# Trainium2: a two-layer transformer trunk whose context part of queries and keys is split first, with the first layer's convolution taps queued behind the query and key chains and the scores of two query tiles issued in turn by parts

## The chip, the cores and the metric

The kernel runs on one core of one Trainium2 chip. The metric is the device time of one execution in microseconds. Engines are named as in the profile: PE is TensorE (matmuls; PEld its weight loads), DVE is VectorE, ACT is ScalarE, POOL is GpSimd, SP is SyncE, which issues most of the DMAs. Each engine works through its own instructions in program order.

## The reference, cut to what matters

Two layers over 256 latent tokens and 256 context tokens of width 1024, all in fp32:

```
h, hc = modulate(rmsnorm(x)), modulate(rmsnorm(ctx))
p, pc = h @ w_in, hc @ w_in                  # GLU | q, k, v | gates
q, k = rope_2d(q), rope_2d(k)                # latent tokens only
conv = (silu(layernorm(dwconv31(glu(p))))) @ w_conv_out
attn = softmax(q k^T over a window + bias, and q k_ctx^T) v  @ w_na_out
x = x + g1 * (sigmoid(gates) . (conv, attn)) @ w_out
x = x + g2 * conv_ffn(modulate(rmsnorm(x)))
# layer 0 does the same for the context; layer 1 only needs its k and v
```

The result must agree with fp32, so every fp32 operand of a large product is split into a high part in the fp32r format and a low part (the rest): three matmuls, high x high, high x low and low x high, stand for one.

## The kernel before, in words

Tokens lie along the free axis (256 latent, then 256 context: 512 columns), channels on the 128 partitions. A "group" is one 128 x 512 output block: eight weight blocks times three matmuls, lines L197 to L199, 24 matmuls of 512 columns. Weights come by SP's DMA (`raw`), and are split on ACT into `whi` (L167 or L216) and on DVE into `wlo` (L168), or for some units of layer 0 on ACT and POOL (L217, L218). There are four buffers of each, so a split for the unit four later can begin when a group has ended. Four PSUM banks (`main`) take group results; two banks `sc`, one `pt` and one `po` belong to the attention.

The mixing half of layer 0 works in this order on PE: query group, key group, two GLU groups; then for each further head pair j = 1, 2, 3 the two GLU groups, the query and the key group; then the 16 gate groups. Between the groups a helper steps through the attention. For a head pair these are the score matmuls of two query tiles (L495), the softmax (L516 adds the bias and takes the maximum on DVE, L519 is the exponential and L522 the scaling on ACT, L521 the reciprocal on DVE), the transposes of the probabilities (L561 on PE, copied out of PSUM by ACT, L564, or L567 for the context), and the products with the values (L578, L587), whose result ACT and DVE split (L595, L596). In layer 0 there are also, after every second pair, the scores of the context's own queries with their softmax (L530, L535, L537, L540).

A query or key "chain" is the DVE and ACT work between a group's end and the scores: two reads of PSUM (L859, L860), the rotation (L861, then L864 for a query, L869 for a key), and splits into high (L881, ACT) and low (L882, DVE). In layer 0 and for keys there is a part that needs no rotation, the context's half of the columns (`qk<-main`).

The depthwise convolution is done on DVE by "taps": 31 instructions for each of four channel blocks, L671 the first and L673 the rest, each adding one shifted, weighted copy to `cb`. They are filler: `conv_run` hands out `rate` of them in each slot, a slot being half a group, in program order between the other work. `conv_tap` puts each behind the DVE instruction in `after[0]`, which before is the latest L516 (or L530). Once all taps are done, DVE adds the four blocks (L949, L950, L951), PE sums them over the channels (L955) and the LayerNorm follows. From the middle of the gate groups on DVE also computes dot products for the modulation (L304).

The score product of one tile is three matmuls for each of two heads, that is three parts:

```
for n, (a, b) in enumerate(((0, 0), (0, 1), (1, 0))):
    for o, r in zip(out, HALF):
        pe.matmul(o, q[r, a, c], runs(k[r, b, d]), start=n == 0, stop=n == 2)
```

with a, b = 0 for the high and 1 for the low part. The two heads use half of the rows each and run side by side.

Of the kernel before, what the change touches and what calls it, by code (L numbers as in the profile page):

```python
# [19 lines left out]
S = 256  # L20
GW = 64
# [32 lines left out]
def trunk(ctx: ExitStack, tc: tile.TileContext, xt, cvec, crow, wall, wada, params, bias_t, rope_t, out):  # L54
    nc = tc.nc
    pe, act, dve, pool, sp = nc.tensor, nc.scalar, nc.vector, nc.gpsimd, nc.sync
# [11 lines left out]
    def nm(s):  # L68
        uid[0] += 1
        return f"{s}_{uid[0]}"  # L70
# [3 lines left out]
    def psum(tag="main"):  # L74
        return psp.tile([P, 512], F32, tag=tag, bufs=BANKS[tag], name=nm(tag))
# [13 lines left out]
    def add_side(gen):  # L89
        side.append(gen)  # L90
# [23 lines left out]
    start = ExitStack()  # L114
# [70 lines left out]
    def runs(a):  # L185

        return a.rearrange("p (r c) -> p c r", r=2)
# [235 lines left out]
    class Attention:  # L423
# [61 lines left out]

        def issue(self):
            _, what, its = self.todo.pop(0)
            outs = [self.products(it, [psum(t) for t in tags]) for it, tags in zip(its, (("sc", "sc"), ("pt", "main")))]
            self.soft.append((what, its, [(self.scores if what == LAT else self.ctx_scores)(it, o) for it, o in zip(its, outs)]))

        def product(self, out, q, k, c, d):

            for n, (a, b) in enumerate(((0, 0), (0, 1), (1, 0))):
                for o, r in zip(out, HALF):
                    pe.matmul(o, q[r, a, c], runs(k[r, b, d]), start=n == 0, stop=n == 2)  # L495

        def products(self, it, out):
            j, qt, q, k, bt = it
            if qt is not None:
                d = slice(0, NS_) if qt else slice(KL, KN)  # L500
                self.product([ps[:, :NS_] for ps in out], q, k, slice(qt * P, (qt + 1) * P), d)
            else:
                for t in range(2):
                    self.product([ps[:, t * S : (t + 1) * S] for ps in out], q, k, slice(S + t * P, S + (t + 1) * P), KCTX)
            return out

        def scores(self, it, out):
            qt, bt = it[1], it[-1]
# [123 lines left out]
    for l in range(DEPTH):  # L632
        last = l == DEPTH - 1
# [4 lines left out]
        with ExitStack() if last else start as e1a:  # L638
# [74 lines left out]
            with ExitStack() as e1b:  # L713
# [123 lines left out]
                    glu_groups(1)  # L837

                conv = conv_run()
                rate[0] = 3 if last else 2.0  # L840
                add_side(conv)

                def qk(j):

                    att.ahead(j - 2)
                    bt = eb.tile([P, 5, NS_ // 2], F32, tag="bias", bufs=2 if last else 1, name=nm("bias"))
                    both = []
                    for what in range(2):
                        w = T if what == 0 else 2 * S
                        sc = HD ** -0.5 if what == 0 else 1.0  # L850
                        ps = in_group((T_Q, T_K)[what] + j, slice(0, w))
                        if what == 0:
# [7 lines left out]
                        dve.stream_shuffle(part(r2[:, LAT]), lat, SWAP16)  # L860
                        dve.tensor_tensor(r2[:, LAT], r2[:, LAT], rope[:, 1, :], ALU.mult)  # L861
                        if what == 0:
                            rq = tmp()
                            dve.tensor_tensor(  # L864
                                rq[:, LAT].rearrange("p (b r c) -> p b r c", b=NB_, r=ROWS),
                                blocks(r1[:, LAT]), blocks(r2[:, LAT]), ALU.add,
                            )
                        else:
                            dve.tensor_tensor(r1[:, LAT], r1[:, LAT], r2[:, LAT], ALU.add)  # L869
                        f = eb.tile([P, 2, KN if what else w], F32R, tag="qk"[what], bufs=2, name=nm("qk"))  # L870
                        if what == 0:
                            to = [([f[:, a, LAT] for a in range(2)], rq[:, LAT])]
                            if T > S:
                                to.append(([f[:, a, CTX] for a in range(2)], ctx_))
                        else:
                            rv_ = r1[:, LAT].rearrange("p (r c) -> p r c", r=ROWS)
                            to = [([f[:, a, KCTX] for a in range(2)], ctx_)]
                            for d, c in ((slice(0, KL), slice(GW - TC, GW)), (slice(KX, KN), slice(0, TC))):
                                to.append(([f[:, a, d].rearrange("p (c r) -> p r c", r=ROWS) for a in range(2)], rv_[:, :, c]))
                        for (hi, lo), src in to:  # L880
                            act.activation(hi, src, AF.Identity, scale=sc)  # L881
                            end = dve.scalar_tensor_tensor(lo, src, sc, hi.bitcast(F32), ALU.mult, ALU.subtract)  # L882
                        both.append(f)
                    att.pair(j, *both, bt, end)

                if l == 0:
                    for t in range(4):
                        keep_v(t, pv[t])
                    qk(0)
                    arun = att.run()  # L890
                    add_side(arun)
                    for j in range(1, 4):
                        glu_groups(j)
                        qk(j)
                        rate[0] = 3
                else:
                    glu_groups(2)
                    rate[0] = 3
                    wvs = [wunit(l, U_V + uu) for uu in range(4)]
                    for half in range(2):  # L900
                        pv = {t: psum() for t in (2 * half, 2 * half + 1)}
                        for k in range(KD):
                            v_tile(pv, wvs[k // 2], k, pv)
                            if k % 2:
                                slot()
                        for t, p in pv.items():
                            keep_v(t, p)
                    qk(0)
                    glu_groups(3)
                    arun = att.run()  # L910
# [446 lines left out]
```

## Time and profile before

| what | value |
|---|---|
| median of 3 runs | 1056.82 us (1056.28 to 1058.88) |
| the profiled execution, its own time | 1054.58 us |
| its span, first to last instruction | 1052.8 us |
| granted TensorE clock, mean | 0.997 |
| busy: PE, DVE, ACT, POOL | 1032.4, 893.2, 565.6, 43.7 us |
| taps: L673 240 times, L671 8 times | 144.7 us for L673 |
| layer 0's mixing half, roughly | 50 to 300 us |
| layer 1's mixing half, roughly | 690 to 850 us |

In a timeline row the first number is the start in microseconds from the span's start, the second the time to the end of the row's last instruction, x the number of instructions merged, and the bracket the idle time of the engine ahead of it with the instruction that ended it. A row of several instructions in a chain gives their spacing.

### The profile page before, as it was taken

What the parts mean: (1) busy time and instruction counts of PE and PEld (TensorE: products, weight loads), DVE (VectorE), ACT (ScalarE), POOL (GpSimd) and SP (SyncE); (2) the same over time, 40 slices, a digit from 0 to 9 for tenths busy, and PEclk for the clock granted to TensorE, in tenths of its full rate; (3) what the DMA queues carried; (4) which work ended last, traced back from release to release, by engine and by line L of the source; (5) the groups of instructions that cost most, each with busy time, mean ns of one, the idle gap of its engine ahead of it and who ended that gap; (6) DMA issues with size and microseconds to landing.
All of it is one profiled execution on the core that took longest, in us unless ns stands there. A gap on an engine that the chain in (4) does not pass through costs nothing.

```text
span 1052.8 us, 17991 instructions
## 1 busy us (share of the span) xinstructions
PE 1032.4 (98%) x6886; PEld 932.9 (89%) x6886; DVE 893.2 (85%) x1608; ACT 565.6 (54%) x921; POOL 43.7 (4%) x59
## 2 busy tenths in 40 slices
PE   9999999999999999999999999999999999999997
PEld 7787788888889988888888889999889999999996
DVE  6568899999998787878788888799899988988883
ACT  4458768545434644444444223545777666766652
POOL 1111110011000000000000000000000000000000
PEclk9999999999999999999999999999999999999998
DMA  9989674888945345454545887556734485666781
GB/s 374 305 221 229 156 181 121 258 255 236 305 146 177 104 140 160 140 164 143 166 145 160 301 289 249 180 189 209 208 123 135 161 292 176 193 201 199 221 283 57
DMA packets 59511, 209.26 MB, mean 199 GB/s; under 512 B 7201, under 2 KB 7457, under 8 KB 59425
## 3 DMA queue, kind: packets, MB, share of 16 engines
q1 hardware_dynamic: 54384, 190.77, 55.3%
q0 software_dynamic: 4752, 17.30, 8.7%
q8 instruction: 54, 0.88, 0.3%
q14 instruction: 33, 0.26, 0.1%
q10 hardware_dynamic: 288, 0.04, 0.0%
HBM read 187.63 MB, written 1.05 MB: 179 GB/s over the span
## 4 chain that ended last, share of the span: by engine, by line
PE 68%; DVE 17%; ACT 5%; DMA 4%; issue 3%; SPq 1%; DVEq 0%; ACTq 0%
PE main L197 20%; PE main L198 20%; PE main L199 20%; DVE cb L673 6%; PE main L736 4%; DVE wlo L168 3%; DMA raw<-in_wall 2%; DVE t L304 2%; DMA own<-in_wada 1%; SPq L728 1%; PE sc L197 1%; PE sc L199 1%; PE sc L198 1%; DVE qk L882 1%; ACT pp L519 1%
## 5 line engine op out<-in xcount | busy, mean ns | idle before, releaser
L197 PE MATMUL main<-h,whi 128*128 128x256 f32 (+1 forms) x1328 | 433.1, 326 | 1.2 <-DVE qk L882 1.2
L198 PE MATMUL main<-h,whi 128*128 128x256 f32 (+1 forms) x1328 | 430.2, 324 | 0.9 <-DVE h L1001 0.7
L199 PE MATMUL main<-h,wlo 128*128 128x256 f32 (+1 forms) x1328 | 429.9, 324 | 1.2 <-DVE wlo L168 1.1
L167 ACT CAST whi<-raw 128x1024 fp32r<-128x1024 f32 (+1 forms) x211 | 218.3, 1039 | 234.8 <-PE main L198 173.6
L168 DVE TENSOR_TENSOR wlo<-raw,whi 128x1024 fp32r<-128x1024 f32 (+1 forms) x211 | 253.6, 1208 | 67.2 <-ACT whi L167 66.4
L197 PEld LDWEIGHTS main<-h,whi 128*128 128x128 f32 x1328 | 252.8, 190 | 22.0 <-issue 1.3
L199 PEld LDWEIGHTS main<-h,wlo 128*128 128x128 f32 x1328 | 252.5, 190 | 18.5 <-DVE wlo L168 1.8
L198 PEld LDWEIGHTS main<-h,whi 128*128 128x128 f32 x1328 | 252.7, 190 | 18.3 <-DVE h L1001 1.0
L304 DVE CUSTOM_DVE_ANT_0 t<-own,sb,par 128x1024 bf16<-128x1024 f32 x120 | 151.8, 1282 | 6.8 <-DMA own<-in_wada 6.8
L673 DVE SCALAR_TENSOR_TENSOR cb<-u,par,cb 128x512 f32<-128x512 f32 (+1 forms) x240 | 144.7, 620 | 2.8
L198 PE MATMUL main<-fl,whi 128*128 128x256 f32 (+1 forms) x396 | 122.8, 310 | 0.0
L197 PE MATMUL main<-fh,whi 128*128 128x256 f32 (+1 forms) x396 | 122.8, 310 | 0.0
L199 PE MATMUL main<-fh,wlo 128*128 128x256 f32 (+1 forms) x396 | 122.5, 310 | 0.0
L197 PEld LDWEIGHTS main<-fh,whi 128*128 128x128 f32 x396 | 75.6, 191 | 3.8 <-ACT fh L1095 0.2
L198 PEld LDWEIGHTS main<-fl,whi 128*128 128x128 f32 x396 | 75.6, 191 | 3.7 <-DVE fl L1096 0.2
L199 PEld LDWEIGHTS main<-fh,wlo 128*128 128x128 f32 x396 | 75.5, 191 | 3.6
L216 ACT CAST whi<-raw 128x1024 fp32r<-128x1024 f32 x33 | 34.6, 1049 | 36.0 <-PE main L198 30.5
L404 ACT ACTIVATE h<-t,mod 128x256 fp32r<-128x256 f32 x56 | 25.2, 503 | 34.8 <-DVE t L403 34.3
L218 POOL DMA_DIRECT2D wlo<-raw x33 | 28.9, 877 | 258.9 <-ACT wlo L217 107.6
L736 PE MATMUL main<-whi,h 128*128 128x512 f32 x128 | 38.5, 386 | 0.2
L1105 ACT ACTIVATE t<-t 128x512 f32<-128x512 f32 x22 | 13.9, 632 | 41.3 <-DVE t L1074 41.3
L217 ACT ACTIVATE wlo<-whi 128x1024 fp32r<-128x1024 f32 x33 | 35.0, 1061 | 0.5
(214 smaller groups left out, 1268.8 us busy)
## 6 DMA issues: line engine op xcount, KB each, us to landing
raw<-in_wall SPq DMA_DIRECT2D x240, 512.0 KB, 4.3
own<-in_wada SPq DMA_DIRECT2D x72, 512.0 KB, 4.7
wlo<-raw POOLq DMA_DIRECT2D x33, 512.0 KB, 5.4
raw<-in_wada SPq DMA_DIRECT2D x16, 512.0 KB, 5.8
bias<-in_bias_t SPq DMA_DIRECT2D x8, 520.0 KB, 5.3
row<-in_wada SPq DMA_DIRECT2D x8, 512.0 KB, 5.1
sb<-in_crow SPq DMA_DIRECT2D x5, 512.0 KB, 4.8
x<-in_xt SPq DMA_DIRECT2D x4, 512.0 KB, 5.1
```

Source lines behind the costliest of these rows:

```text
L167: act.copy(hi[:, c], r[:, c])
L168: dve.tensor_tensor(lo[:, c], r[:, c], hi[:, c].bitcast(F32), ALU.subtract)
L197: pe.matmul(ps, w[0], order(xh), start=start, stop=False)
L198: pe.matmul(ps, w[0], order(xl), start=False, stop=False)
L199: pe.matmul(ps, w[1], order(xh), start=False, stop=stop)
L216: act.copy(hi, r)
L217: act.mul(lo, hi.bitcast(F32), -1.0)
L218: pool.dma_start(lo, r, accum_op=ALU.add)
L304: dve.tensor_tensor_reduce(tmp().bitcast(BF16), r, v, 1.0, pr(l, BADA + n, 1), ALU.mult, ALU.add, mods[l][:, n, s : s + 1])
L404: high = act.activation(hi[:, c], y[:, c], AF.Identity, bias=b)
L673: dve.scalar_tensor_tensor(cb[j], src, w, cb[j], ALU.mult, ALU.add)
L736: mm = pe.matmul(pv[t], h1[n == 1][k][:, c], runs(w[n == 2][:, b]), start=k + n == 0, stop=k == KD - 1 and n == 2)
```

## The change

Five things change, and no instruction is added or removed on any engine.

1. In `qk`, the context's part of a query or key is split (ACT, then DVE) right behind the two reads of PSUM, ahead of the rest of the rotation, by a new helper `parts`.
2. Of the two windows of a key, the one that the first query tile needs is split first.
3. In layer 0 `after[0]` is set to the end of each chain, so that taps handed out during a chain are queued behind it, and not inside. In layer 1 it isn't.
4. In layer 0 the tap rate is 1.5 while a pair's chains are issued, 3 behind them and 4 behind the last pair (before: 2, and 3 from the second pair on).
5. The scores of a head pair are issued by parts: part 0 of both tiles, part 1 of both, part 2 of both, and the parts are now high x high, low query x high key, high query x low key.

```
         def issue(self):
             _, what, its = self.todo.pop(0)
-            outs = [self.products(it, [psum(t) for t in tags]) for it, tags in zip(its, (("sc", "sc"), ("pt", "main")))]
+            outs = [[psum(t) for t in tags] for tags in (("sc", "sc"), ("pt", "main"))]
+            if what == LAT:
+                for part in range(3):
+                    for it, out in zip(its, outs):
+                        self.products(it, out, part)
+            else:
+                for it, out in zip(its, outs):
+                    self.ctx_products(it, out)
...
+        def product(self, out, q, k, c, d, n):
+
+            for o, r in zip(out, HALF):
+                a, b = ((0, 0), (1, 0), (0, 1))[n]
+                pe.matmul(o, q[r, a, c], runs(k[r, b, d]), start=n == 0, stop=n == 2)
...
+                def parts(f, d, src, sc, view=lambda a: a):
+                    hi, lo = (view(f[:, a, d]) for a in range(2))
+                    act.activation(hi, src, AF.Identity, scale=sc)
+                    return dve.scalar_tensor_tensor(lo, src, sc, hi.bitcast(F32), ALU.mult, ALU.subtract)
...
                     att.ahead(j - 2)
+                    if not last:
+                        rate[0] = 1.5
...
                         dve.stream_shuffle(part(r2[:, LAT]), lat, SWAP16)
+                        f = eb.tile([P, 2, KN if what else w], F32R, tag="qk"[what], bufs=2, name=nm("qk"))
+                        if ctx_ is not None:
+                            parts(f, KCTX if what else CTX, ctx_, sc)
                         dve.tensor_tensor(r2[:, LAT], r2[:, LAT], rope[:, 1, :], ALU.mult)
...
-                            for d, c in ((slice(0, KL), slice(GW - TC, GW)), (slice(KX, KN), slice(0, TC))):
-                                to.append(([f[:, a, d].rearrange("p (c r) -> p r c", r=ROWS) for a in range(2)], rv_[:, :, c]))
...
+                            for d, c in ((slice(KX, KN), slice(0, TC)), (slice(0, KL), slice(GW - TC, GW))):
+                                end = parts(f, d, rv_[:, :, c], sc, lambda a: a.rearrange("p (c r) -> p r c", r=ROWS))
+                        if not last:
+                            after[0] = end
                         both.append(f)
                     att.pair(j, *both, bt, end)
+                    rate[0] = 4.0 if j == 3 and not last else 3.0
```

Where instructions stand now, at three places.

DVE in layer 0, from the key chain of the second head pair (j = 1) to its first L516. Before, with `main_943` the key group's result and `cb_0` the first channel block of the convolution:

```order
L859 TENSOR_TENSOR t_1012<-main_943,rope_196 128x256
L860 STREAM_SHUFFLE t_1013<-main_943 128x256
L673 SCALAR_TENSOR_TENSOR cb_0_184<-u_0_197,par,cb_0_184 128x512
L861 TENSOR_TENSOR t_1013<-t_1013,rope_196 128x256
L882 SCALAR_TENSOR_TENSOR qk_1018<-main_943,qk_1018 128x256
L869 TENSOR_TENSOR t_1012<-t_1012,t_1013 128x256
L673 SCALAR_TENSOR_TENSOR cb_0_184<-u_0_197,par,cb_0_184 128x512 x2
L882 SCALAR_TENSOR_TENSOR qk_1018<-t_1012,qk_1018 128x4x40 x2
L673 SCALAR_TENSOR_TENSOR cb_0_184<-u_0_197,par,cb_0_184 128x512 x3
L516 ISA sc_1063,mx_1079<-sc_1063,bias_893 128x2x208
```

The same stretch after the change, where the lines are L874, L875, L879, L887 and L854 for the chain, L681 for the tap and L524 for L516:

```order
L874 TENSOR_TENSOR t_1012<-main_944,rope_196 128x256
L875 STREAM_SHUFFLE t_1013<-main_944 128x256
L879 TENSOR_TENSOR t_1013<-t_1013,rope_196 128x256
L887 TENSOR_TENSOR t_1012<-t_1012,t_1013 128x256
L854 SCALAR_TENSOR_TENSOR qk_1016<-main_944,qk_1016 128x256
L854 SCALAR_TENSOR_TENSOR qk_1016<-t_1012,qk_1016 128x4x40 x2
L681 SCALAR_TENSOR_TENSOR cb_0_184<-u_0_197,par,cb_0_184 128x512 x6
L524 ISA sc_1063,mx_1079<-sc_1063,bias_895 128x2x208
```

Three taps have left the chain, and six in place of three stand between its end and the softmax. In the query chain ahead of it (not shown) there are five taps before and three after; the taps up to this L516 are 30 in both.

DVE in layer 0, from the last L516 of the fourth head pair to the first L530 of the second context softmax. Before:

```order
L516 ISA mx_1781 128x1
L673 SCALAR_TENSOR_TENSOR cb_2_186<-u_2_199,par,cb_2_186 128x512 x2
L521 RECIPROCAL ri_1778<-sm_1776 128x1
L673 SCALAR_TENSOR_TENSOR cb_2_186<-u_2_199,par,cb_2_186 128x512
L521 RECIPROCAL ri_1786<-sm_1784 128x1
L673 SCALAR_TENSOR_TENSOR cb_2_186<-u_2_199,par,cb_2_186 128x512 x4
L168 TENSOR_TENSOR wlo_2160<-raw_2158,whi_2159 128x1024
L673 SCALAR_TENSOR_TENSOR cb_2_186<-u_2_199,par,cb_2_186 128x512 x5
L596 TENSOR_TENSOR ol_2_194<-po_1902,oh_2_190 128x4x4x16
L530 TENSOR_REDUCE mx_343_1945<-sc_1917 128x2
```

After (L604 is L596, L538 is L530, L529 is L521):

```order
L524 ISA mx_1771 128x1
L681 SCALAR_TENSOR_TENSOR cb_2_186<-u_2_199,par,cb_2_186 128x512 x2
L529 RECIPROCAL ri_1768<-sm_1766 128x1
L681 SCALAR_TENSOR_TENSOR cb_2_186<-u_2_199,par,cb_2_186 128x512
L529 RECIPROCAL ri_1776<-sm_1774 128x1
L681 SCALAR_TENSOR_TENSOR cb_2_186<-u_2_199,par,cb_2_186 128x512 x3
L168 TENSOR_TENSOR wlo_2159<-raw_2157,whi_2158 128x1024
L681 SCALAR_TENSOR_TENSOR cb_2_186<-u_2_199,par,cb_2_186 128x512 x10
L604 TENSOR_TENSOR ol_2_194<-po_1896,oh_2_190 128x4x4x16
L538 TENSOR_REDUCE mx_343_1939<-sc_1911 128x2
```

Sixteen taps stand there in place of twelve. Of all 124 taps of layer 0 the L516 of the fourth pair has 78 ahead of it before and 68 after; this L530 has 90 and 84; so 34 taps lie between it and L951 before, and 40 after.

DVE in layer 1, the softmax of the second head pair with the key chain of the third inside it (`main_7438` is the key group's result). Before:

```order
L516 ISA mx_7532 128x1
L861 TENSOR_TENSOR t_7557<-t_7557,rope_6578 128x256
L521 RECIPROCAL ri_7529<-sm_7527 128x1
L516 ISA pt_7516,mx_7540<-pt_7516,bias_7210 128x2x208
L516 ISA mx_7540 128x1
L521 RECIPROCAL ri_7537<-sm_7535 128x1
L516 ISA main_7517,mx_7548<-main_7517,bias_7210 128x2x208
L516 ISA mx_7548 128x1
L869 TENSOR_TENSOR t_7556<-t_7556,t_7557 128x256
L882 SCALAR_TENSOR_TENSOR qk_7562<-main_7438,qk_7562 128x256
```

After:

```order
L524 ISA mx_7532 128x1
L854 SCALAR_TENSOR_TENSOR qk_7560<-main_7438,qk_7560 128x256
L529 RECIPROCAL ri_7529<-sm_7527 128x1
L524 ISA pt_7510,mx_7540<-pt_7510,bias_7210 128x2x208
L524 ISA mx_7540 128x1
L529 RECIPROCAL ri_7537<-sm_7535 128x1
L524 ISA main_7511,mx_7548<-main_7511,bias_7210 128x2x208
L524 ISA mx_7548 128x1
L879 TENSOR_TENSOR t_7557<-t_7557,rope_6578 128x256
```

The split of the context's part, the last reader of that PSUM bank, has moved ahead of the rest of the softmax.

On PE only the score matmuls change places among themselves, in both layers, and L955 now stands two matmuls of a group later. On ACT the high splits of the rotated part move ahead of a weight split or of a softmax at five places, and the gate's L711 moves ahead of a weight split (L167) in the second context softmax. SP's queue keeps its order but for one bias load, which goes behind one weight load.

More of the change, by code (lines that the diff above doesn't have):

```diff
@@ L487, in issue, with products, ctx_products @@
             _, what, its = self.todo.pop(0)
-            outs = [self.products(it, [psum(t) for t in tags]) for it, tags in zip(its, (("sc", "sc"), ("pt", "main")))]
-            self.soft.append((what, its, [(self.scores if what == LAT else self.ctx_scores)(it, o) for it, o in zip(its, outs)]))
[L491 to L497, printed above, removed]
-            j, qt, q, k, bt = it
[L499 to L505, printed above, removed]
+            outs = [[psum(t) for t in tags] for tags in (("sc", "sc"), ("pt", "main"))]
[6 more added lines that the diff above has]
+                    self.ctx_products(it, out)
+            self.soft.append((what, its, [(self.scores if what == LAT else self.ctx_scores)(it, o) for it, o in zip(its, outs)]))
+        def product(self, out, q, k, c, d, n):
+            for o, r in zip(out, HALF):
+                a, b = ((0, 0), (1, 0), (0, 1))[n]
+                pe.matmul(o, q[r, a, c], runs(k[r, b, d]), start=n == 0, stop=n == 2)
+        def products(self, it, out, n):
+            j, qt, q, k, bt = it
+            d = slice(0, NS_) if qt else slice(KL, KN)
+            self.product([ps[:, :NS_] for ps in out], q, k, slice(qt * P, (qt + 1) * P), d, n)
+        def ctx_products(self, it, out):
+            j, _, q, k, _ = it
+            for t in range(2):
+                for n in range(3):
+                    self.product([ps[:, t * S : (t + 1) * S] for ps in out], q, k, slice(S + t * P, S + (t + 1) * P), KCTX, n)
         def scores(self, it, out):
@@ L869, in qk @@
                             dve.tensor_tensor(r1[:, LAT], r1[:, LAT], r2[:, LAT], ALU.add)
-                        f = eb.tile([P, 2, KN if what else w], F32R, tag="qk"[what], bufs=2, name=nm("qk"))
                         if what == 0:
-                            to = [([f[:, a, LAT] for a in range(2)], rq[:, LAT])]
-                            if T > S:
-                                to.append(([f[:, a, CTX] for a in range(2)], ctx_))
+                            end = parts(f, LAT, rq[:, LAT], sc)
                         else:
                             rv_ = r1[:, LAT].rearrange("p (r c) -> p r c", r=ROWS)
-                            to = [([f[:, a, KCTX] for a in range(2)], ctx_)]
-                            for d, c in ((slice(0, KL), slice(GW - TC, GW)), (slice(KX, KN), slice(0, TC))):
-                                to.append(([f[:, a, d].rearrange("p (c r) -> p r c", r=ROWS) for a in range(2)], rv_[:, :, c]))
-                        for (hi, lo), src in to:
-                            act.activation(hi, src, AF.Identity, scale=sc)
-                            end = dve.scalar_tensor_tensor(lo, src, sc, hi.bitcast(F32), ALU.mult, ALU.subtract)
+                            for d, c in ((slice(KX, KN), slice(0, TC)), (slice(0, KL), slice(GW - TC, GW))):
+                                end = parts(f, d, rv_[:, :, c], sc, lambda a: a.rearrange("p (c r) -> p r c", r=ROWS))
+                        if not last:
+                            after[0] = end
                         both.append(f)
                     att.pair(j, *both, bt, end)
+                    rate[0] = 4.0 if j == 3 and not last else 3.0
                 if l == 0:
@@ L894, in trunk @@
                         qk(j)
-                        rate[0] = 3
                 else:
```

2 lines of the change are left out of this document (1 added, 1 removed).

## The prediction

> **What bounds the kernel now.** I read the page's first part, then a table of busy time by stretch, then the timeline of each engine around the places where PE waits. The page's first rows:
>
> ```profile
> span 1052.8 us, 17991 instructions
> PE 1032.4 (98%) x6886; PEld 932.9 (89%) x6886; DVE 893.2 (85%) x1608; ACT 565.6 (54%) x921; POOL 43.7 (4%) x59
> ```
>
> PE is busy all but 20.4 us of the span, and the change leaves its matmuls as they are. So the time moves only by what PE waits, and every term below is a wait of PE that grows or shrinks. The stretches (from and to, length, then busy time of PE, PEld, DVE, ACT, POOL, then the granted clock, the DMA share and GB/s):
>
> ```profile
> 60.00:157.00 97.00, 93.22 (x590) 77.96 (x589) 84.26 (x188) 69.42 (x136) 13.38 (x16) 1.00 0.81 199
> 157.00:212.00 55.00, 54.88 (x355) 46.05 (x354) 51.85 (x88) 36.04 (x73) 3.98 (x5) 1.00 0.66 188
> 300.00:400.00 100.00, 100.00 (x648) 92.95 (x647) 83.02 (x148) 47.42 (x73) 1.41 (x2) 1.00 0.46 147
> ```
>
> PE's waits of layer 0's mixing half lie ahead of 157. From there to 212 DVE is busy 51.85 of 55 us: it runs through its list almost without a pause, so what is put ahead of an instruction there delays it in full. From 300 to 400 PE is busy all of the time: what is won or lost before is neither given back nor made up there. The profiled execution (1054.58 us, 1.8 of it outside the span) is 2.24 below the median of the runs, 1056.82. I sum against the profiled one and add 2.24. A measurement of this kernel can tell about 0.3% from no change, which is 3.2 us: faster means under 1053.65, slower over 1059.99.
>
> **What a tap costs by its neighbours.** Two rows of DVE's timeline, six taps on alternating `cb` and five on one, and two neighbours from a query chain:
>
> ```profile
> 135.65 4.06 DVE L673 SCALAR_TENSOR_TENSOR cb<-u,par,cb 128x512 f32<-128x512 f32 x6
> 166.29 3.90 DVE L673 SCALAR_TENSOR_TENSOR cb<-u,par,cb 128x512 f32<-128x512 f32 x5
> 87.42 0.74 DVE L673 SCALAR_TENSOR_TENSOR cb<-u,par,cb 128x512 f32<-128x512 f32 x1
> 88.09 0.45 DVE L860 STREAM_SHUFFLE t<-main 128x256 f32<-128x256 f32 x1
> ```
>
> A tap alone takes 0.74. The five on one accumulator start (3.90 - 0.74) / 4 = 0.79 apart, the six alternating ones (4.06 - 0.74) / 5 = 0.66. The tap at 87.42 ends at 88.16, and the L860 behind it, which doesn't need it, starts at 88.09. So a tap costs 0.66 beside independent work and 0.79 behind a tap on the same accumulator. The Trainium skill ("VectorE: DVE Perf Modes", "The DRAIN you can't avoid") says that the next operation on this engine doesn't start until the pipe is empty, though one that isn't held starts earlier; the first half, taken alone, gives 0.74 or more in either neighbourhood, against the rows above. By that half the six taps of place 4 would cost 6 x 0.74 rather than 6 x 0.66 and lose the 0.5 credited there, and the sum would be 1.0 higher.
>
> **Place 1: scores of the second pair (j = 1), about 96.** DVE, then one row of ACT:
>
> ```profile
> 94.41 0.42 DVE L869 TENSOR_TENSOR t<-t,t 128x256 f32<-128x256 f32 x1
> 94.74 1.54 DVE L673 SCALAR_TENSOR_TENSOR cb<-u,par,cb 128x512 f32<-128x512 f32 x2
> 96.20 0.81 DVE L882 SCALAR_TENSOR_TENSOR qk<-t,qk 128x160 fp32r<-128x160 f32 x2
> 96.91 2.33 DVE L673 SCALAR_TENSOR_TENSOR cb<-u,par,cb 128x512 f32<-128x512 f32 x3
> 99.16 0.59 DVE L516 CUSTOM_DVE_ANT_0 sc<-sc,bias 128x416 f32<-128x416 f32 x1
> 95.20 0.79 ACT L881 ACTIVATE qk<-t 128x160 fp32r<-128x160 f32 x2
> ```
>
> and PE:
>
> ```profile
> 96.04 0.44 PE L495 MATMUL sc<-qk,qk 64*128 64x416 f32 x2 [0.87 <-ACT qk L881]
> 97.07 0.62 PE L495 MATMUL sc<-qk,qk 64*128 64x416 f32 x4 [0.58 <-DVE qk L882]
> 98.14 0.48 PE L197 MATMUL main<-h,whi 128*128 128x512 f32 x1
> 104.94 1.08 PE L578 MATMUL po<-pT,V 128*64 128x256 f32 x8
> ```
>
> PE waits 0.87 and 0.58 here. Three taps leave the chain (1.54 of them stands between L869 and L882) and two others the query chain, so the scores end about 1.9 earlier (an estimate: 0.87 + 0.58 + about 0.45 of score matmuls that no longer stand behind the second wait). But L516 at 99.16 follows the taps and not the scores: three taps stand right ahead of it, and six after the change. Of the taps ahead of it since 77 it loses two that now fill idle time ahead of 84 (-1.3), it gains DVE's waits for ACT in the two chains that no tap fills now (an estimate of 0.7 for each, from L869's end at 94.83 to L881's first half at about 95.6: +1.4), and taps on one accumulator that now follow each other, nine more of them at 0.13 (+1.1). L516 comes about 1.2 later, and the values, which PE reaches at 104.94, with it. PE: **+1.2** at this place; bounds -1.9 (L516 not late) and +1.9 (no tap fills earlier idle time). I take +1.2, since six taps (4.5 us) stand between the chain and L516 and none of the waits ahead of it ends later.
>
> **Place 2: scores of the third pair, 128.6.** ACT and PE:
>
> ```profile
> 125.32 0.81 ACT L881 ACTIVATE qk<-t 128x160 fp32r<-128x160 f32 x2 [1.58 <-DVE t L869]
> 125.91 1.07 ACT L216 CAST whi<-raw 128x1024 fp32r<-128x1024 f32 x1
> 127.02 1.06 ACT L217 ACTIVATE wlo<-whi 128x1024 fp32r<-128x1024 f32 x1
> 127.98 1.05 ACT L567 COPY pT<-sc 128x512 f32<-128x512 f32 x2
> ...
> 129.40 0.61 ACT L567 COPY pT<-main 128x512 f32<-128x512 f32 x1
> ...
> 128.60 1.28 PE L495 MATMUL sc<-qk,qk 64*128 64x416 f32 x6 [1.69 <-ACT pT L567]
> 129.72 0.34 PE L495 MATMUL main<-qk,qk 64*128 64x416 f32 x1
> 130.07 0.34 PE L495 MATMUL main<-qk,qk 64*128 64x416 f32 x1
> ```
>
> PE waits 1.69 for L567, which frees `sc` behind two weight splits, and these stand behind L881, for which ACT waited 1.58 until DVE came past its taps to L869. That wait goes: -1.6. Given back: +0.35, since the second tile's bank (`main`) is copied out last, at 129.40, and the parts in turn need it after two matmul pairs, which leaves five pairs behind it and not three, at (130.07 - 129.72) / 2 = 0.175 each. With 0.15 for the place 1 lateness that goes on, PE gains 1.1: it stands at **+0.1** (bounds -1.5 and +1.2). At the fourth pair, by the same reasoning with shorter waits, -0.3: **-0.2**.
>
> **Place 3: the second context softmax.** DVE from the last L516 on, and who waits:
>
> ```profile
> 159.76 1.54 DVE L673 SCALAR_TENSOR_TENSOR cb<-u,par,cb 128x512 f32<-128x512 f32 x2
> 170.41 0.42 DVE L596 TENSOR_TENSOR ol<-po,oh 128x256 fp32r<-128x256 f32 x1 [0.22 <-ACT oh L595]
> 170.75 1.28 DVE L530 TENSOR_REDUCE mx<-sc 128x2 f32<-128x512 f32 x2
> 177.49 1.06 ACT L167 CAST whi<-raw 128x1024 fp32r<-128x1024 f32 x1
> 178.42 0.93 ACT L540 ACTIVATE pp<-pp,ri 128x256 f32<-128x256 f32 x2
> 179.74 1.08 PE L578 MATMUL po<-pT,V 128*64 128x256 f32 x8
> ```
>
> From 159.76 to L530 stand twelve taps, sixteen after the change: 4 x 0.79 = +3.2. Off that go 0.22 (L596 no longer waits for ACT) and 0.5 (the fourth pair's softmax begins earlier, 0.2 with PE and 0.3 by its own chain): L530 comes at +2.4. PE reaches the values at 179.74 without a wait, right behind ACT's L540, so it waits for the lateness. L711 ahead of the L167 adds 0.5 on ACT's way to L540 (half of its 1.06, the other half I take as hidden), and 0.1 is hidden by the transposes. PE stands at **+2.8**; bounds 0 (DVE enters 2.4 earlier) and +4.
>
> **Place 4: the end of the convolution.**
>
> ```profile
> 212.27 0.69 DVE L951 TENSOR_TENSOR ss<-ss,cb 128x512 f32<-128x512 f32 x1
> 211.67 0.38 PE L199 MATMUL main<-h,wlo 128*128 128x512 f32 x1
> 213.02 1.12 PE L955 MATMUL po<-ss,one 128*128 128x512 f32 x2 [0.97 <-DVE ss L951]
> ```
>
> PE already waits 0.97 for L951. Six more taps lie between L530 and it: 6 x 0.66 = 4.0, less 0.5 (four pairs fewer on one accumulator), less 0.6 (DVE's wait for a DMA ahead of the first L304 at 196, covered by the delay) = +2.85. With L530's +2.4 L951 comes at 212.27 + 5.25 = 217.5. L955 stands two matmuls later, which takes 0.4 of it. As this wait is the last, it sets what layer 0 costs, and places 1 to 3 count through it only: PE stands at **+4.85**. Bounds: +6.6 if place 1's lateness reaches here; below, -4.3 (first rival).
>
> **Layer 1.** No tap moves behind a chain here; the readers of the key's bank come earlier:
>
> ```profile
> 761.65 0.45 PE L197 MATMUL main<-h,whi 128*128 128x512 f32 x1 [0.55 <-DVE qk L882]
> 777.14 0.38 PE L197 MATMUL main<-h,whi 128*128 128x256 f32 x1 [0.63 <-DVE qk L882]
> ```
>
> Both waits go, -1.2; parts in turn give back 0.35 at one of the two later pairs (the trace shows no such order; 0 to 0.7). **-0.8**; bounds -1.9 (all score waits of the three pairs shorter) and +0.6 (both give back and the softmax is split by L854).
>
> **Free**: the key window that is split first, the bias load behind one weight load (DMA share 0.81 and below) and the order of the high and low parts (same matmuls) change no wait that I see; if the bias load came late, one L516 would wait, under 1 us.
>
> **Sum.** 1054.58 + 4.85 - 0.8 = 1058.6 in a profiled execution, 2.24 more as median: **1060.9 us**.
>
> **Rivals.** *Faster: DVE keeps up.* Chains without taps let the scores and so the next groups come earlier, and DVE's pauses (97.00 - 84.26 = 12.7 us from 60 to 157) get the taps. Then place 1 gives -1.9, place 2 -1.1, the fourth pair -0.2, and the wait of 0.97 with 0.1 beside it goes: -4.3, with layer 1 -5.1: 1049.5, median 1051.7. It decides at L951: for PE to gain all of that, L951 must come by 208.4; faster by over 0.3% needs it by 210.3. For it: those 12.7 us. Against it: 94% busy from 157 on and the lower rate of 1.5. Chance 0.26. *Same: half the lateness.* If six taps behind place 1's chain push L516 by nothing and DVE comes to L530 1.2 late and finds its idle time shorter on the way, L951 comes near 215, +2.7 - 0.4 - 0.8 = +1.5: 1058.3. Chance 0.17. *Nothing: banks and buffers hold the scores.* If the scores at 96 and 128 wait for PSUM (as for L567 at 128.60) and not for the chains, neither gain nor lateness comes, and layer 1's -0.8 is left: 1056.0. For it the 1.69 above; against it 0.87 and 0.58, which name L881 and L882. Chance 0.07.
>
> **How the numbers follow.** The forecast has 0.50, with a range of its own from 1058.4 to 1064.0 (bounds of places 3 and 4): 0.36 of that is over 1059.99. Faster: 0.24 of the first rival. Same: 0.14 + 0.02 + 0.17 + 0.07 = 0.40. As cases of both signs hold much of the chance, the range goes from the first rival's 1051.5 to 1064.0.
>
> **What would show it.** Right: PE's waits at 96 and 97 gone, L516 of the second pair near 100.4, L530 near 173, the wait ahead of L955 above 2 us, L951 near 217.5, and in layer 1 no wait for the low split at 761 and 777. Wrong: L951 at 212 or earlier, or L516 of the second pair ahead of 99; then DVE has found room for the taps, and the first rival is the case. If PE's waits ahead of 157 are as long as now, the third is.

## The result, and the profile after

The changed kernel takes 1067.58 us in the median of six runs (1065.87 to 1070.42), the kernel before 1057.56 (1054.91 to 1059.01): a ratio of 1.0098, with a 95% interval of 1.0079 to 1.0116. It is slower, as forecast, by 10 us and not by 4. The profiled execution took 1065.87 us. One execution of a later run (experiment 6) took 1330.7 us at a granted clock of 0.75 and is left out everywhere. The page of the profiled one begins:

```profile
span 1064.1 us, 17991 instructions
PE 1036.4 (97%) x6886; PEld 934.2 (88%) x6886; DVE 898.6 (84%) x1608; ACT 565.1 (53%) x921; POOL 43.5 (4%) x59
```

The span grew by 11.3 us and PE's busy time by 4, with the same matmuls. Where it went is found by comparing when PE starts the same group in the two traces:

| first matmul of the group behind | before | after | PE late by | forecast |
|---|---|---|---|---|
| the scores of the second pair | 98.14 | 96.80 | -1.3 | -1.9 |
| its values (place 1) | 108.49 | 110.10 | +1.6 | +1.2 |
| place 2, third pair | 130.34 | 130.45 | +0.1 | +0.1 |
| the fourth pair's scores | 155.65 | 155.39 | -0.3 | -0.2 |
| place 3, second context softmax | 185.88 | 190.82 | +4.9 | +2.8 |
| place 4, L955, and one group more | 219.16 | 230.78 | +11.6 | +4.85 |
| end of PE's last instruction | 1046.21 | 1057.50 | +11.3 | +4.05 |

Up to 156 us the working holds within 0.6 us, and all that was missed in layer 0 lies between 156 and 231. Behind that the lag stays near 11.5: next to nothing is given back or lost. DVE after, at the places of the rows of before:

```profile
96.19 4.67 DVE L681 SCALAR_TENSOR_TENSOR cb<-u,par,cb 128x512 f32<-128x512 f32 x6
100.77 0.59 DVE L524 CUSTOM_DVE_ANT_0 sc<-sc,bias 128x416 f32<-128x416 f32 x1
...
173.71 1.28 DVE L538 TENSOR_REDUCE mx<-sc 128x2 f32<-128x512 f32 x2
...
181.10 6.70 DVE L681 SCALAR_TENSOR_TENSOR cb<-u,par,cb 128x512 f32<-128x512 f32 x10
...
189.37 1.22 DVE L168 TENSOR_TENSOR wlo<-raw,whi 128x1024 fp32r<-128x1024 f32 x1
...
203.38 1.28 DVE L304 CUSTOM_DVE_ANT_0 t<-own,sb,par 128x1024 bf16<-128x1024 f32 x1 [4.15 <-ACT g L719]
...
222.25 0.69 DVE L964 TENSOR_TENSOR ss<-ss,cb 128x512 f32<-128x512 f32 x1
```

L538 (L530 before) comes at 173.71, 2.96 later than before; L964 (L951) at 222.25, 9.98 later. From the one to the other before took 212.27 - 170.75 = 41.5 us, after 48.5. Of these 7.0, 3.55 are one wait, and the 3.5 that are left are the six more taps: DVE stood 4.15 us ahead of the first dot product L304, and before 0.60:

```profile
196.55 1.28 DVE L304 CUSTOM_DVE_ANT_0 t<-own,sb,par 128x1024 bf16<-128x1024 f32 x1 [0.60 <-DMA own<-in_wada]
```

The row of after names ACT's L719, which is no operand of L304; the operand that can be late is the load `own`. In experiment 4, where the order is the same but for the taps in the chains, the row of the same wait (4.13) names `own`. The rows of before that matter for it, of DVE, PE and SP's queue:

```profile
178.80 1.22 DVE L168 TENSOR_TENSOR wlo<-raw,whi 128x1024 fp32r<-128x1024 f32 x1
184.00 1.95 PE L578 MATMUL sc<-pT,V 128*64 128x256 f32 x16
180.05 0.33 SPq L164 DMA_DIRECT2D raw<-in_wall  x1
186.03 0.80 SPq L282 DMA_DIRECT2D sb<-in_crow  x2
186.88 2.46 SPq L154 DMA_DIRECT2D own<-in_wada  x4
```

SP's queue after:

```profile
190.65 0.33 SPq L164 DMA_DIRECT2D raw<-in_wall  x1
191.09 0.85 SPq L282 DMA_DIRECT2D sb<-in_crow  x2
191.98 2.62 SPq L154 DMA_DIRECT2D own<-in_wada  x4
```

The load of a weight unit (L164) stands ahead of `sb` and `own`, and it waits until the L168 of 189.37 has read the buffer that it fills. That L168 has moved behind the ten taps of 181.10, and before it ran at 178.80. There is a second gate: `sb` takes over memory of the attention, and before the change it was issued at 186.03, 0.08 us behind the end of the last values (184.00 + 1.95 = 185.95). After it, these values end at 188.94 + 1.95 = 190.89, late with place 3. Both gates open within 0.3 us of each other. So `own` is issued 5.1 us later, and lands 11.3 instead of 9.5 us after its issue; why it takes longer isn't shown (in experiment 2, behind the same loads, it took 9.0). PE's rows after, from place 3 to place 4:

```profile
179.75 0.27 PE L569 MATMUL pt<-ident,pp 64*128 64x64 f32 x1 [0.91 <-ACT pp L548]
...
182.43 0.27 PE L569 MATMUL pt<-ident,pp 64*128 64x64 f32 x1 [1.88 <-ACT pp L548]
...
183.34 1.97 PE L586 MATMUL po<-pT,V 128*64 128x256 f32 x8
...
188.94 1.95 PE L586 MATMUL sc<-pT,V 128*64 128x256 f32 x16
...
223.00 2.08 PE L968 MATMUL po<-ss,one 128*128 128x512 f32 x2 [5.41 <-DVE ss L964]
...
225.29 0.63 PE L197 MATMUL main<-h,whi 128*128 128x512 f32 x1
225.72 0.63 PE L198 MATMUL main<-h,whi 128*128 128x512 f32 x1
```

The wait ahead of L968 (L955) is 5.41 us where it was 0.97. And the matmuls behind it start 0.43 apart, twice the usual 0.215, until 227. The eight values at 183.34 take 1.97 us for what took 1.08 in the rows of before. The granted clock says the same (third number from the end, 1.00 is full speed), after from 157 on, then before at the place of the long wait:

```profile
157.00:212.00 55.00, 51.87 (x332) 42.86 (x330) 48.57 (x85) 33.40 (x69) 2.59 (x3) 0.97 0.57 156
212.00:224.00 12.00, 6.59 (x27) 4.96 (x26) 11.79 (x17) 3.66 (x5) 0.89 (x1) 0.85 0.92 264
224.00:232.00 8.00, 8.00 (x30) 6.42 (x29) 6.97 (x13) 3.66 (x6) 0.00 (x0) 0.80 0.39 120
```

```profile
212.00:224.00 12.00, 11.03 (x50) 9.27 (x50) 11.95 (x19) 6.33 (x9) 0.87 (x1) 1.00 0.83 244
```

So L964 is late by 10.0 and PE by 11.6. From the start of L955 to the next group PE took 219.16 - 213.02 = 6.14 us before and 230.78 - 223.00 = 7.78 after, though two matmuls fewer (0.43) stand there now: the slow clock behind the long wait costs 2.07 us, and the two matmuls give 0.4 of it back.

### The profile page after: what moved, and what is told of

Its sections match the earlier page's. It is cut to its first block, busy times and chain, and to the rows that moved or that the text cites. A ratio compares the mean times of both kernels' runs of the same rounds, so it can differ in the third digit from the quotient of the medians.

```text
span 1064.1 us, 17991 instructions
## 1 busy us (share of the span) xinstructions
PE 1036.4 (97%) x6886; PEld 934.2 (88%) x6886; DVE 898.6 (84%) x1608; ACT 565.1 (53%) x921; POOL 43.5 (4%) x59
## 4 chain that ended last, share of the span: by engine, by line
PE 78%; DVE 13%; ACT 5%; DMA 3%; issue 2%; DVEq 0%; SPq 0%; ACTq 0%
PE main L197 23%; PE main L198 23%; PE main L199 22%; PE main L744 4%; DVE cb L681 4%; DVE wlo L168 2%; DMA raw<-in_wall 2%; ACT whi L167 1%; PE sc L199 1%; DVE t L304 1%; PE sc L197 1%; PE sc L198 1%; DMA sb<-in_crow 1%; PE po L230 1%; DVE t L1012 1%
## 5 line engine op out<-in xcount | busy, mean ns | idle before, releaser
L167 ACT CAST whi<-raw 128x1024 fp32r<-128x1024 f32 (+1 forms) x211 | 217.8, 1037 | 235.0 <-PE main L198 163.6
L168 DVE TENSOR_TENSOR wlo<-raw,whi 128x1024 fp32r<-128x1024 f32 (+1 forms) x211 | 253.5, 1206 | 68.3 <-ACT whi L167 68.0
L304 DVE CUSTOM_DVE_ANT_0 t<-own,sb,par 128x1024 bf16<-128x1024 f32 x120 | 151.6, 1279 | 10.8 <-DMA own<-in_wada 6.6
L681 DVE SCALAR_TENSOR_TENSOR cb<-u,par,cb 128x512 f32<-128x512 f32 (+1 forms) x240 | 144.3, 618 | 3.7
```

The lines of the kernel that those rows point to most:

```text
L167: act.copy(hi[:, c], r[:, c])
L168: dve.tensor_tensor(lo[:, c], r[:, c], hi[:, c].bitcast(F32), ALU.subtract)
L304: dve.tensor_tensor_reduce(tmp().bitcast(BF16), r, v, 1.0, pr(l, BADA + n, 1), ALU.mult, ALU.add, mods[l][:, n, s : s + 1])
L681: dve.scalar_tensor_tensor(cb[j], src, w, cb[j], ALU.mult, ALU.add)
```

## The experiments

The theory: the loss is made by where the rates put the taps between 156 and 222, on DVE's list ahead of L964. The main rival: taps behind the chains (`after[0] = end`), or the chains and scores themselves. Each ratio is to the kernel before in runs on the same chip, with its 95% interval; "profiled" is the one execution with a trace, to be held against 1054.58 and 1065.87. That trace of before is 3.0 us below the median of its six, and the traces of experiments 11 and 12, whose ratios show no change, are 5.2 and 5.1 us longer than it. So a lag of PE in one trace tells where time goes, and the ratio how much.

**1. Only the rates, first try.**

```
+                    if not last:
+                        rate[0] = 1.5
                     bt = eb.tile(...)
...
                     att.pair(j, *both, bt, end)
+                    rate[0] = 4.0 if j == 3 and not last else 3.0
```

> Before with the tap rates of after (1.5 in the chains, 3 behind them, 4 behind the last pair) and nothing else. Theory: slow by itself, since 66 in place of 78 taps stand ahead of the fourth pair's L516 and 105 in place of 96 ahead of the L168 that holds SP's queue: 7 to 14 us over before, 1065 to 1072, with a wait of DVE of 3 us or more ahead of the first L304. Rival, the chains: 1056 to 1060.

Measured: 1059.36 us, ratio 1.0026 (1.0007 to 1.0044), profiled 1058.14. A miss, and first of all one of the experiment: the loop that calls `qk` in the kernel before sets the rate to 3 directly behind it, so 4 was never in force, and L955 stood 36 matmuls later on PE than in either kernel. L951 and PE's wait there:

```profile
219.91 0.69 DVE L954 TENSOR_TENSOR ss<-ss,cb 128x512 f32<-128x512 f32 x1
```

```profile
220.65 1.13 PE L958 MATMUL po<-ss,one 128*128 128x512 f32 x2 [2.90 <-DVE ss L954]
```

L951 is late by 7.6 us, but not by the wait that the theory wants: L304 doesn't wait here, and 46 taps and eight dot products stand between L530 and L951 in place of 34 and six. And PE has 36 matmuls more to do in that time and waits 2.90 rather than 5.41. The expectation looked at DVE's list alone; where the waiting matmul stands decides as much.

**2. Only the rates, as the changed kernel has them.** As above, and the line `rate[0] = 3` in the loop taken out.

> Before with the tap rates of after as the changed kernel really runs them: 1.5 in the chains, 3 behind them and 4 behind the last pair, so that 68 taps stand ahead of the fourth pair's L516, 101 ahead of the L168 and L955 stands where it does in before. (In the run with the rates only, the loop set 3 again at once behind the last pair; there L955 stood 36 matmuls later.) Theory: the rates alone carry most of the loss, place 3 with a wait of 2 us or more at about 180, DVE's wait for the first L304 over 3 us, L955 waiting over 4 us: 1063 to 1069. Rival, the rates lose only together with taps behind the chains: 1056 to 1060.

Measured: 1065.24 us, ratio 1.0077 (1.0056 to 1.0097), profiled 1064.91.

```profile
202.09 1.29 DVE L304 CUSTOM_DVE_ANT_0 t<-own,sb,par 128x1024 bf16<-128x1024 f32 x1 [2.77 <-DMA own<-in_wada]
...
220.95 0.69 DVE L953 TENSOR_TENSOR ss<-ss,cb 128x512 f32<-128x512 f32 x1
```

```profile
187.03 1.95 PE L578 MATMUL sc<-pT,V 128*64 128x256 f32 x16
...
221.70 2.07 PE L957 MATMUL po<-ss,one 128*128 128x512 f32 x2 [5.84 <-DVE ss L953]
```

```profile
190.75 0.33 SPq L164 DMA_DIRECT2D raw<-in_wall  x1
191.18 1.74 SPq L282 DMA_DIRECT2D sb<-in_crow  x2
```

The rates alone, in the kernel before, make 8 of the 10 us, with waits at the same places: 0.83 and 1.40 at place 3 (where the values then run at full speed), 2.77 ahead of L304, 5.84 ahead of L955. DVE's wait for `own` was 0.2 us under the 3 expected. Here the queue is seen by itself: the attention's last matmuls end at 188.98, which would have let `sb` go, and SP comes to it at 191.18, behind the weight load.

**3. The rates of before in the changed kernel** (2, and 3 from the second pair on; all else as changed).

> After with the tap rates of before (2, then 3 from the second pair on), taps still behind the chains. Theory: the loss comes from where the taps stand from 160 to 212, which the rates set; with 78 and 96 taps ahead of the fourth pair's L516 and of the L168 on which SP's queue waits, as before the change, L951 comes within 2 us of its 212 and the wait ahead of L955 falls from 5.4 to under 2.5: 1055 to 1059. Rival, taps behind the chains are the cause: within 3 us of the changed kernel's 1067.6.

Measured: 1060.02 us, ratio 1.0020 (1.0003 to 1.0036), profiled 1059.75. One us above the range expected.

```profile
216.87 0.69 DVE L962 TENSOR_TENSOR ss<-ss,cb 128x512 f32<-128x512 f32 x1
```

```profile
217.62 1.12 PE L966 MATMUL po<-ss,one 128*128 128x512 f32 x2 [1.01 <-DVE ss L962]
```

The wait ahead of L955 is back to 1.01 and no clock is lost. L951 isn't at 212 but at 216.9, since PE is 3.7 us late already at the fourth pair's scores and DVE with it: what is left of the change loses about 2 us by itself (1.0003 to 1.0036), in this one trace at the second and the fourth pair. About 7.5 of the 10 us go with the rates.

**4. Taps inside the chains again** (the two lines that set `after[0]` out, rates as changed).

> After without the two lines that set after[0], so that taps stand inside the chains again; rates as in after. Theory: the count of taps ahead of each softmax stays (48, 68), so the loss stays: 1064 to 1070. Rival, taps behind the chains are the cause: 1056 to 1060.

Measured: 1065.26 us, ratio 1.0074 (1.0052 to 1.0096), profiled 1065.01; DVE's wait for `own` 4.13, PE's ahead of L955 5.41, both as in the changed kernel. The rival has fallen: most of the loss stays without it. The median is 2.3 us below that of the changed kernel, but the two intervals overlap, so whether the taps' place behind the chains costs anything isn't settled.

**5. Rate 3 behind the last pair in the changed kernel.**

```
-                    rate[0] = 4.0 if j == 3 and not last else 3.0
+                    rate[0] = 3.0
```

> After with 3 in place of 4 behind the last pair: 12 taps and not 16 ahead of the second context softmax's first maximum, L955 36 matmuls later on PE. Theory: place 3's wait shrinks to under 1.5 us, the attention's memory comes free near 186 and the first L304 waits under 1 us, L955 finds its sum nearly ready: 1057 to 1061. Rival, chains and scores by parts carry the loss: 1063 to 1068.

Measured: 1062.82 us, ratio 1.0054 (1.0037 to 1.0071), profiled 1062.76, between the two ranges.

```profile
171.00 1.28 DVE L538 TENSOR_REDUCE mx<-sc 128x2 f32<-128x512 f32 x2
...
222.20 0.69 DVE L964 TENSOR_TENSOR ss<-ss,cb 128x512 f32<-128x512 f32 x1
```

```profile
186.25 0.80 SPq L282 DMA_DIRECT2D sb<-in_crow  x2
187.11 2.21 SPq L154 DMA_DIRECT2D own<-in_wada  x4
```

```profile
222.95 1.12 PE L968 MATMUL po<-ss,one 128*128 128x512 f32 x2 [2.90 <-DVE ss L964]
...
256.44 0.48 PE L199 MATMUL main<-oh,wlo 128*128 128x512 f32 x1 [2.11 <-DMA wlo<-raw]
```

Place 3 is mended (L538 at 171.00, PE no longer waits there), `own` stands ahead of the weight load in SP's queue and L304 doesn't wait. But six more taps and two more dot products stand between L538 and L964, which is at 222.20 as in the changed kernel. PE waits 2.11 at 256 for a low weight part that a DMA of POOL makes; it was issued at 245.87:

```profile
245.87 0.92 POOL L218 DMA_DIRECT2D wlo<-raw  x1 [5.51 <-ACT wlo L217]
```

Between 331 and 342 PE loses about 2 us more, in short waits. Mended places gave way to others; what makes the last two isn't shown.

**6. `sb` and `own` loaded by ACT's queue** instead of SP's.

> After with the loads of the modulation's weights and vectors (sb, own) issued by ACT and not by SP, so that they do not stand behind the weight load for which SP waits until the late L168. Theory A, the load waits for the attention's memory, that is for the last L586, late by 5 us: the first L304 still waits 1.5 to 3.5 us, 1063 to 1067. Theory B, it waits for SP's queue: the wait falls under 1 us, L964 comes 3.5 us earlier and the time is 1060 to 1063.

Measured: 1064.20 us in the median of three executions (1063.08 to 1064.61), ratio 1.0069 (1.0043 to 1.0095), profiled 1063.08. It doesn't decide between its theories: ACT came to `own` only at 201.62, behind its own wait for the second `sb`, and the first L308 (L304) waited 3.59:

```profile
206.41 1.28 DVE L308 CUSTOM_DVE_ANT_0 t<-own,sb,par 128x1024 bf16<-128x1024 f32 x1 [3.59 <-DMA own<-in_wada]
```

What the rows of the changed kernel settle is that either gate would have been enough there: the memory comes free at 190.89, and `sb` was issued at 191.09. Without the queue it could have gone at most 0.2 us earlier, and without the late values not at all, since in experiment 2 too SP takes 0.43 from the weight load to `sb`. Experiment 2 shows the queue holding the load alone, by 2 us, and experiment 5 shows both gates open (`sb` at 186.25) and no wait.

**7. Eight more operations between L951 and L955**, in the kernel before.

```
                     dve.tensor_tensor(sm[:, :T], sm[:, :T], flat[3], ALU.add)
+                    if not last:
+                        for _ in range(8):
+                            dve.tensor_scalar(sm[:, :T], sm[:, :T], 1.0, 0.0, ALU.mult, ALU.add)
```

> Before with eight more DVE operations in a row between L951 and L955, each a multiplication of the sum by 1.0 in place: about 8 x 0.58 = 4.6 us. Theory: PE's wait ahead of L955 grows from 0.97 by all of it to about 5.6 and nothing is given back later; and as after the changed kernel's wait of 5.4, the next matmuls run 0.43 apart for some 3 us, 1.6 us more: 1062.5 to 1065, +6.2. Rival, the slow matmuls have another cause: +4.6. Rival, PE or DVE make it up later: under +2.

Measured: 1061.72 us, ratio 1.0049 (1.0030 to 1.0069), profiled 1060.55.

```profile
212.66 0.69 DVE L951 TENSOR_TENSOR ss<-ss,cb 128x512 f32<-128x512 f32 x1
213.39 3.65 DVE L954 TENSOR_SCALAR ss<-ss 128x512 f32<-128x512 f32 x8
```

```profile
217.10 1.58 PE L958 MATMUL po<-ss,one 128*128 128x512 f32 x2 [4.12 <-DVE ss L954]
...
218.90 0.63 PE L198 MATMUL main<-h,whi 128*128 128x512 f32 x1
```

This is 0.8 us below the range, since the eight took 3.65 and not 4.6 us. PE's wait grew by 3.15, and the matmuls behind it are slow. PE was 1.0 behind already since 108; the group at L955 starts 4.1 us later than in before, the one behind it 5.8, and 6.0 is still there at the end. So lateness of L951 reaches the end in full, and a wait of 4 us costs 1.7 us of clock on top: 3.65 + 1.7 = 5.35, and the ratio gives 5.2.

**8. Dot products held back until L955 is issued**, in the changed kernel.

```
-                    pace[0] = 0.5
+                    pace[0] = 0.0
...
-                    pace[0] = 1.0 if last else 1.2
+                    if last:
+                        pace[0] = 1.0
...
                     (s2,) = sum_squares(1, T)
+                    if not last:
+                        pace[0] = 2.0
```

> After, with the modulation's dot products (L304) held back until L955 is issued and then handed out at 2.0 in place of 1.2, so that no dot product and no wait for its weights stands ahead of L964 on DVE. Theory: L964's lateness is what the dot products, their wait and the taps make on DVE: without some 3.6 us of wait and 8 us of dot products it comes near 210, PE doesn't wait for it, the slow matmuls go too, and what is left is place 3 with about 4 us: 1057 to 1062. Rival, PE's wait is made by something else (the convolution's own length): 1064 or more.

Measured: 1071.83 us, ratio 1.0137 (1.0112 to 1.0162), profiled 1070.93. A miss in the time, with the mechanism as expected up to 245:

```profile
214.03 0.69 DVE L965 TENSOR_TENSOR ss<-ss,cb 128x512 f32<-128x512 f32 x1
```

```profile
218.69 1.02 PE L969 MATMUL po<-ss,one 128*128 128x512 f32 x2
...
253.44 0.48 PE L199 MATMUL main<-h,wlo 128*128 128x512 f32 x1 [3.47 <-DVE wlo L168]
```

The sum is ready 8.2 us earlier, PE doesn't wait for it, no clock is lost, and PE runs 5.6 us behind the kernel before rather than 11.6. Then the dot products crowd DVE, L168 comes late, and PE's lag grows from 5.6 to 16.7 between 247 and 270.

**9. and 10. The same in the kernel before, with the rates of experiment 1 and alone**, two tries at a kernel faster than both.

> Before with the rates 1.5 and 3 and the dot products held back until L955 is issued, then at 2.0. Theory: the rates alone brought PE 2 us ahead at 186 and lost it ahead of L955; with a shorter list ahead of it that stays, if the dot products still come in time for the next half: 1053 to 1056. Rival, the dot products come late or crowd DVE from 215 to 330: 1058 to 1062.

> Before with only the dot products held back in that way. Theory: the wait of 0.97 ahead of L955 goes, 1055.5 to 1056.5; rival, the dot products come late: 1058 to 1061.

Measured: 1082.41 us (1.0234, 1.0210 to 1.0257) and 1067.25 us (1.0095, 1.0077 to 1.0113). Both miss. In the second L951 is done at 205.48 and L955 doesn't wait, which gains 1.3, and PE's lag then goes from 0.1 at 240 to 12.1 at 270. No version that was run beats the kernel before.

**11. Only the order of the chain; 12. only the scores by parts**, each in the kernel before.

> Before with the order of the chain alone (context's part first, first window first): rates, taps inside the chains and scores as in before. Theory: within 1.5 us of before in layer 0; in layer 1 the two waits for L882 (0.55, 0.63) go, but PE then reaches the scores while their PSUM banks still wait for ACT's copy, so nothing is left of it: 1055.5 to 1058.5. Rival, the forecast's layer 1 term: -0.8.

> Before with only the scores issued by parts of the two tiles in turn. Theory: worth little, since the second tile's bank is the last to come free: within 1 us of before, 1056 to 1058. Rival: a gain of 1 us or more.

Measured: 1058.53 us (1.0011, 0.9995 to 1.0028) and 1057.13 us (1.0004, 0.9984 to 1.0024): neither is told from no change. Layer 1 is answered by the changed kernel's own trace and the first of these. PE's scores of the third pair, and ACT's copy that frees their bank, before:

```profile
769.37 1.05 PE L495 MATMUL sc<-qk,qk 64*128 64x416 f32 x6
```

```profile
768.73 0.85 ACT L564 COPY pT<-sc 128x384 f32<-128x384 f32 x2
```

and after:

```profile
780.69 0.82 PE L502 MATMUL sc<-qk,qk 64*128 64x416 f32 x2 [0.44 <-ACT pT L572]
```

```profile
780.17 0.85 ACT L572 COPY pT<-sc 128x384 f32<-128x384 f32 x2
```

In both the scores start 0.5 to 0.6 us behind the start of the copy. The 0.7 us that PE wins at 761 brings it to a bank that is not free: it waits 0.44 there, and by the next group all of the gain is lost. In the kernel with the chain's order alone it is the same, with 0.61 ahead of the same scores.

## Why the prediction was wrong, by its steps

- **Places 1 and 2, and the fourth pair: right.** L516 of the second pair came at 100.77 (forecast 100.4), PE's lag by 1.6, 0.1 and -0.3 (1.2, 0.1, -0.2). The waits at 96 and 97 shrank to one of 0.39. The price of a tap by its neighbours held: 6 taps in a row took 4.67 us, (4.67 - 0.74) / 5 = 0.79 apart.
- **Place 3: mechanism right, too small.** L530 late by 2.96 for 2.4: the last L516 came 0.13 later and not 0.5 earlier. ACT's last L548 came another 0.5 late, as forecast, but by luck: the sum took half of a 1.06, and that is L167, which stood on this way before too; what came new is the gate's L719, 0.48 from its start to the next. PE waited 0.91 and 1.88 in two pieces and then ran at half clock through the values, which wasn't in the sum: +4.9 for +2.8.
- **Place 4: the step that failed** is "less 0.6 (DVE's wait for a DMA ahead of the first L304 at 196, covered by the delay)". The sum held that load fixed while DVE came later. In the run DVE reaches L304 3.3 us later (its taps end at 199.23 for 195.95) and the load comes 6.8 later: 5.1 in its issue, held by both gates, and 1.7 in its landing. The weight load ahead of it in SP's queue waits for an L168 that stands 17 taps behind the first L530 of that softmax, before 6, and no term of the sum followed it to SP; the memory comes free with place 3, which was 4.9 late and not 2.8. The wait became 4.15 in place of nothing: 4.15 of the 4.75 us by which L951 was later than forecast (222.25 for 217.5). The six taps were right (3.5 with their neighbours, forecast 3.5).
- **The clock was missing** as a term: 2.0 us behind the wait of 5.41. The 0.4 that two matmuls more ahead of L955 take was right. 4.75 + 2.0 = 6.75 is the difference between +4.85 and +11.6.
- **Layer 1: wrong, small.** -0.8 forecast; PE's lag went from 11.6 at 658 (time of before) to 11.4 at 824. The two waits for L882 did go, and the banks took their place, which is the mechanism of the third rival, in the other layer.
- **The first rival** (DVE fills its pauses) didn't happen: from 60 to 157 DVE's idle time grew from 12.7 to 14.2 us. After the change (the stretch as in the prediction):

```profile
60.00:157.00 97.00, 93.53 (x590) 78.23 (x589) 82.80 (x178) 69.53 (x136) 13.84 (x16) 1.00 0.80 198
```

## What to carry to other kernels

When filler work is moved on a busy engine, follow every instruction that falls behind it, not only the softmax at hand: a weight split that frees a buffer holds a DMA queue, and what stands behind in that queue may be an operand of the same busy engine. A wait at the end of such a list costs by two numbers, when the producer is done and how much work stands ahead of the consumer on its own engine; a change of rate moves both. Do not credit a delay with covering a DMA until it is seen which gates let that DMA go, the queue and the memory that it fills, and whether the same change moves them too.

## What the runs showed of the hardware

PE's matmuls of 512 columns start 0.215 us apart, and 0.427 for a while behind a long wait. Ahead of L955, waits of 0.97, 2.26 (experiment 6) and 2.90 us were followed by none of these, waits of 4.12, 5.41 and 5.84 by two to five of them behind one of 1.2 us, for 1.6 to 2.1 us in all. In experiments 8 and 10 waits of 3.47 and 3.37, each 4 us behind a shorter one (1.02 and 0.78), were followed by seven and nine. Several waits close together can do it too: in the kernel with the chain's order alone, the waits at 129 and 131 (1.58 and 0.62, with short ones between) slow the group behind them, while 1.08 and 1.30 at 103 and 105 in the changed kernel did not. A slow one (a usual one takes 0.38 in such a row):

```profile
133.10 0.63 PE L198 MATMUL main<-h,whi 128*128 128x512 f32 x1
```

The Trainium skill ("TensorE: Matmul & The Clock Gate", "Part 1: The HAM clock gate (the "warmup" mystery)") says that PE's clock is halved after an idle window of about 3.4 us, that it takes about as long of work to come back, and that the windows run freely, so that the point varies. The traces agree on the half speed (0.427 for 0.215) and on a limit between 2.9 and 4.1 us for a single wait ahead of L955. The slow stretch lasted about 4 us behind L968 (223.0 to 227), near what the page gives.

Eight operations on 128x512 in place, each on the result of the one ahead, took 3.65 us, 0.45 apart, less than taps on one accumulator (0.79) or on two (0.66).
